# Two-layer decoder trunk (gated linear attention, then sparse attention) on one core: products ahead of the first weights, grouped activation functions, other pacing of the top-k, and embedding blocks and last-head values in other places

## The chip, the cores and the metric

The kernel runs on one core of a Trainium2 chip. The time is the device time of one execution in microseconds (us). Three executions of the kernel before took 2016.35, 2017.49 and 2019.79 us; their median is 2017.49 us.

The engines of the core work side by side, each in the order in which its instructions were issued: PE (TensorE, matrix products), ACT (ScalarE, activation functions and copies), DVE (VectorE, elementwise work), POOL (GpSimd) and SP (SyncE, which here only issues DMAs). They wait for one another through semaphores.

## The reference

Two layers over 1024 tokens of width 1024, in float32. Cut to what matters here:

```python
# layer 0: gated linear attention, 4 heads, chunks of 64 tokens
h = x @ w_in                                   # q, k, v, z, a
g = log_sigmoid(a @ w_a2 + b_a) / 16           # decay per channel
G = cumsum(g, within a chunk)
q_t, k_t = q * dk**-0.5 * exp(G), k * exp(-G)
o = tril(q_t k_t^T) v + q_t S                  # S carried from chunk to chunk
y0 = (rms(o) * gn_g * silu(z)) @ w_out
# layer 1: an indexer scores all keys, 256 of them are kept, 16 heads
score = sum_h relu(qi_h . ki) * wi_h           # causal
idx   = top_k(score, 256)
o     = softmax(q k[idx]^T * scale) v[idx]
y1    = (o * silu(z)) @ w_out
# behind each mixer
x = LayerNorm(alpha * x + y_i)
x = x + (p[i] @ W_ple) * sigmoid(x @ W_gate)
```

## The kernel before

**Numbers.** Nearly every operand of a product is split into a high part (rounded to fp32r) and a low part (the rest), and a product is three matmuls: hi·hi, hi·lo, lo·hi. `split` makes the high part on ACT (L403) and the low one on DVE (L395). The weights are loaded from HBM into "wst" and split into "whi" (ACT, L180) and "wlo" (DVE, L182) by the class `Weights` (`W`), in the order of the list `seq`; `take` hands out the next pair. Weights that are used in both halves of the tokens are split once, ahead, by `split_ahead` (ACT L219, DVE L223, through "pst" and "phi") into HBM, and loaded whole later (`whi<-whs`).

**Stages.** The 1024 tokens are worked in two halves of 512. For layer 0, a half runs through four heads: v, a, z, q and k projections, the decay (`g_phase`), the chunks (`core_steps`), and the output product (`out_phase`), then the normalization and `tail`: transposes of y, the embedding product p W_ple ("ple", 8 blocks of 6 matmuls 128x512), and 8 gate blocks of 24 matmuls. Behind half 0 of layer 0 stand keys, values and the indexer (`small_head`, `index_steps`, `small_kv`). Layer 1 has 17 slots in a half (plan of `slots()`): in slot h the scores S of head h+1 are made, and the values ("o", `pv`) of head h are summed, between projections ("q", "z") and output products ("o" units) that fill PE. The last output units (`last_outs`), the normalization and `tail` end the half.

**What sets the order.** The program is written in the order of the matmuls. `Flow` keeps a clock `now` that counts the columns of the matmuls issued so far at 2.4 GHz. Everything else is put on a heap with a due time (`at`, `after`, `chain`, `spread`) and issued when the clock passes it; `need` runs the heap until something is there. Three pacers run beside it: `W` (a step of the weights every 1.15), `bg` (the top-k and others, a step every `gap`), and `bg3` (`split_ahead`). So the due times fix the order on ACT, DVE and SP, and a wait at run time holds all that stands behind it on its engine.

**The places that the change touches:**
- Start (L1177 on): the first loads and splits of x and of the v weights. `ident` (L356) is the identity that transposes use.
- `g_phase` (L511): on ta [128, 2, 512], per half of the channels Exp (L513), Ln (L514), then a scan; `decays` is another Exp (L539, L541, L542) for the two halves. `z_phase` uses Silu (L602). A change of function set puts an ACT_TABLE_LOAD ahead of the activation.
- `accumulate` (L734) adds an output product into y on DVE (L760, L762) and calls `norm` per token block in its second pass: `stats` (two bn_stats of 512 columns, L803, and bn_aggr, L804), POOL's power for 1/std, and `apply` (L808).
- `load_p` loads the half's p and splits it behind `wait`.
- Index stage: `rl` (L1022, ACT) is the relu of an index product "ix", `sc` (L1016, L1018, DVE) its weighted sum; `zz` (L984) a value evacuation that PE's transposes `U<-ident,zz` wait for; `feed_by` the x splits of half 1.
- Top-k (`topk_steps`): a search by bits, one step every 1.6. A step is a count on DVE (L1040, "tk" or "tkj") or ACT (L1084). At the last bit three score tiles are loaded back (`sc<-sc_s`, L1077) and counted on DVE at 768, 896 and 1024 columns.
- `attend`: `parts` makes ph and PT (the high and low probabilities, L1481 ACT and L1479 DVE), `inverse` and `to_all` bring 1/sum to all partitions by way of HBM (`row`, L1499, and `inv<-row`, L1507), and `pv`, in its last group, multiplies z by inv (L1524), then the values by z (`uf`, L1533), and splits uf into the u of the output product (L403, L395).

Of the kernel before, what the change touches and what calls it, by code (L numbers as in the profile page):

```python
# [23 lines left out]
HT = 512  # L24
NK = 8
# [112 lines left out]
class Weights:  # L138
# [15 lines left out]
    def step(self):  # L154
# [110 lines left out]
def trunk_kernel(ctx, tc, x_tok, x_T, p_T, pos, freq, g_q, g_k, g_v, g_z, g_a, g_a2, g_ba, g_gn, g_o,  # L265
# [28 lines left out]
    def tail_keys(layer):  # L294
        return ([(("p", layer, c), ple_c[layer, c]) for c in range(2)]
                + [(("t", layer, b), gate_c[layer, b]) for b in range(NK)])
# [36 lines left out]
    last_outs = [("o", (6,), 1), ("o", (7,), 0), ("o", (7,), 1)]  # L333

    def unit_keys(u):
        if u[0] == "o":
# [157 lines left out]
    def g_phase(u, A):  # L494
# [16 lines left out]
        def soft(d):  # L511
            def f():
                act.activation(ta[:, d], ta[:, d], AF.Exp, scale=-1.0)  # L513
                act.activation(ta[:, d], ta[:, d], AF.Ln, bias=1.0)  # L514
            return f
# [29 lines left out]
        chain((0, lambda: None), (0.6, soft(0)), (1.1, soft(1)), (0.3, scan(0)), (1.1, scan(1)),  # L545
              (0.8, middle), (1.9, decays))
# [193 lines left out]
    def accumulate(parts, U, y, ch, rs=None, norm=None, ahead=1):  # L740
# [5 lines left out]
        for t, b in order:  # L746
# [16 lines left out]
            if norm is not None:  # L763
                norm(t)
            yield

    def out_phase(u, y, norm=None):
# [4 lines left out]
        for ch in range(2):  # L772
            parts = [W.take(("o", u["h"], ch, 0)), W.take(("o", u["h"], ch, 1))]
            for i, _ in enumerate(accumulate(parts, U, y, ch, u["rs"], norm if ch else None)):
# [14 lines left out]
    def norm_steps(y, np_, eps):  # L789
# [6 lines left out]
        def norm(t):  # L796
# [3 lines left out]

            def stats():
                for c in range(2):
                    dve.bn_stats(st8[:, t, c], y[:, t, c * 512:c * 512 + 512])  # L803
# [944 lines left out]
```

## Time and profile before

| | |
|---|---|
| three runs | 2016.35, 2017.49, 2019.79 us |
| the profiled execution | 2016.59 us, of which the span is 2014.8 us |
| TensorE clock granted, mean | 0.993 |
| share of the span in 40 slices | PE 9 tenths or more in all but two (8) |
| POOL busy | 53.7 us (3%) |
| ACT_TABLE_LOADs | 57 |

A row of the trace's timeline reads: start and duration in us, engine, line, operation, output<-input, shape, how many instructions it holds, and in brackets the idle time that the engine had ahead of it and what ended that wait. The durations of matmuls overlap, so what one costs is the distance between starts. A row of the view by lines has busy us and mean ns behind the bar.

### The profile page before, as it was taken

To read this page: it belongs to the slowest core of one execution; us is meant where nothing else is said; L and a number is where in the kernel's file an instruction comes from. 1 tells how busy PE (TensorE), PEld (TensorE's weight loads), DVE (VectorE), ACT (ScalarE), POOL (GpSimd) and SP (SyncE) were. 2 spreads that over 40 slices of the span, in tenths; PEclk is the share of its full clock that TensorE was granted. 3 is DMA by queue.
4 is the path that set the end of the run, shared out by engine and by line. 5 is a ranking of instruction groups with operands and counts; after the bars stand their busy time and mean duration, and the time that the engine had idled before them with its cause. 6 is when DMAs were issued, how large, how long until landed. Compare 5 with 4: busy or idle time off the path is not lost.

```text
span 2014.8 us, 26716 instructions
## 1 busy us (share of the span) xinstructions
PE 1963.4 (97%) x9016; PEld 1616.3 (80%) x9016; DVE 1487.6 (74%) x3037; ACT 1046.5 (52%) x1943; POOL 53.7 (3%) x111
## 2 busy tenths in 40 slices
PE   8999999999999999999999999999899999999999
PEld 6788788877777888888888887888778888888877
DVE  5667666687677797877867986777796887777863
ACT  5664646445465646464555676766442553434432
POOL 0000000010000000000100000000000000000000
PEclk9999999999999999999999999999999999999999
DMA  4557575657856565657667487877766998888864
GB/s 149 174 162 221 171 218 171 222 174 243 283 180 224 161 225 167 225 162 224 196 218 266 157 311 246 303 265 276 271 211 215 352 333 295 291 300 279 295 249 147
DMA packets 173947, 464.96 MB, mean 231 GB/s; under 512 B 20081, under 2 KB 20849, under 8 KB 167665
## 3 DMA queue, kind: packets, MB, share of 16 engines
q1 hardware_dynamic: 173808, 463.25, 68.4%
q8 instruction: 71, 1.16, 0.2%
q14 instruction: 68, 0.55, 0.1%
HBM read 331.18 MB, written 131.99 MB: 230 GB/s over the span
## 4 chain that ended last, share of the span: by engine, by line
PE 81%; DVE 7%; ACT 5%; DMA 4%; issue 2%; SPq 0%; POOL 0%; POOLq 0%; ACTq 0%; DVEq 0%
PE pb L58 59%; PE o L58 8%; PE U L58 6%; PE S L58 5%; DMA xst<-x2s 1%; DMA wls<-pst 1%; DMA pst<-in_d_o 1%; DVE bn L803 1%; PE oT L62 1%; PE tr L58 1%; DVE wlo L182 1%; DVE sc L1018 1%; ACT whi L180 0%; DMA wst<-in_g_v 0%; DMA wlo<-wls 0%
## 5 line engine op out<-in xcount | busy, mean ns | idle before, releaser
L58 PE MATMUL pb<-x,whi 128*128 128x512 f32 x2272 | 709.9, 394 | 3.3 <-ACT whi L180 2.0
L58 PEld LDWEIGHTS pb<-x,whi 128*128 128x128 f32 x2272 | 417.2, 188 | 84.4 <-ACT whi L180 2.8
L58 PE MATMUL pb<-x,wlo 128*128 128x512 f32 x1136 | 444.2, 391 | 0.4 <-DVE wlo L182 0.4
L58 PE MATMUL pb<-whi,u 128*128 128x512 f32 x1024 | 347.2, 399 | 7.6 <-DVE u L395 4.2
L58 PEld LDWEIGHTS pb<-x,wlo 128*128 128x128 f32 x1136 | 213.8, 188 | 48.1 <-DVE wlo L182 2.3
L58 PEld LDWEIGHTS pb<-whi,u 128*128 128x128 f32 x1024 | 194.8, 190 | 49.9 <-DVE u L395 5.0
L58 PE MATMUL pb<-wlo,u 128*128 128x512 f32 x512 | 202.3, 395 | 0.0
L182 DVE TENSOR_TENSOR wlo<-wst,whi 128x512 fp32r<-128x512 f32 x232 | 154.8, 684 | 56.2 <-ACT whi L180 56.0
L180 ACT ACTIVATE whi<-wst 128x512 fp32r<-128x512 f32 x232 | 136.4, 621 | 47.2 <-DMA wst<-in_g_z 13.7
L219 ACT ACTIVATE phi<-pst 128x512 fp32r<-128x512 f32 x130 | 81.4, 626 | 126.2 <-DMA pst<-in_d_z 40.8
L1435 ACT ACTIVATE sq<-P,mx 128x128 f32<-128x128 f32 (+7 forms) x128 | 99.0, 774 | 83.8 <-DVE mx L1428 56.5
L1481 ACT ACTIVATE ph<-PT 128x512 fp32r<-128x512 f32 (+1 forms) x160 | 93.7, 601 | 65.7 <-PE o L58 50.4
L58 PE MATMUL S<-kT,q 128*128 128x512 f32 (+2 forms) x576 | 121.8, 343 | 0.0
L1479 DVE TENSOR_TENSOR PT<-PT,ph 128x512 fp32r<-128x512 f32 (+1 forms) x160 | 101.5, 648 | 20.6 <-ACT ph L1481 20.6
L58 PEld LDWEIGHTS S<-kT,q 128*128 128x128 f32 x576 | 100.6, 188 | 17.8 <-DVE mx L1428 0.7
L58 PEld LDWEIGHTS pb<-wlo,u 128*128 128x128 f32 x512 | 97.6, 191 | 18.8
L223 DVE TENSOR_TENSOR pst<-pst,phi 128x512 fp32r<-128x512 f32 x130 | 89.1, 685 | 29.8 <-ACT phi L219 29.8
L1084 ACT ACTIVATE tk<-sc,tki 128x768 f16<-128x768 f32 (+2 forms) x90 | 92.9, 1032 | 22.0 <-DVE tki L1093 15.9
L58 PE MATMUL o<-ph,vT 128*128 128x512 f32 (+2 forms) x384 | 102.4, 351 | 0.0
L1441 DVE STREAM_TRANSPOSE sq<-sq 128x128 f32<-128x128 f32 (+7 forms) x128 | 97.6, 768 | 3.1 <-ACT sq L1435 3.0
L58 PE MATMUL pb<-whi,x 128*128 128x512 f32 x256 | 89.1, 407 | 10.0 <-ACT whi L180 6.0
L709 ACT ACTIVATE junk<-o 128x512 bf16<-128x512 f32 x32 | 19.1, 597 | 139.8 <-DVE ot L707 135.3
(311 smaller groups left out, 3383.9 us busy)
## 6 DMA issues: line engine op xcount, KB each, us to landing
whi<-whs SPq DMA_DIRECT2D x130, 512.0 KB
wlo<-wls SPq DMA_DIRECT2D x130, 512.0 KB
sqd<-sq SPq DMA_DIRECT2D x192, 256.0 KB
PT<-sqd SPq DMA_DIRECT2D x48, 1024.0 KB
whs<-phi SPq DMA_DIRECT2D x130, 256.0 KB
wls<-pst SPq DMA_DIRECT2D x130, 256.0 KB
wst<-in_g_v SPq DMA_DIRECT2D x32, 512.0 KB
wst<-in_g_z SPq DMA_DIRECT2D x32, 512.0 KB
```

The source lines that it names most:

```text
L58: self.pe.matmul(out, lhsT, rhs, start=start, stop=stop)
L62: self.pe.transpose(out, in_, ident)
L180: self.nc.scalar.activation(hi[:, c], st[:, c], AF.Copy, scale=1.0 if gain is None else gain)
L182: self.nc.vector.tensor_sub(lo[:, c], st[:, c], hi[:, c].bitcast(F32))
L219: self.nc.scalar.activation(hi, st.bitcast(F32), AF.Copy)
L223: self.nc.vector.tensor_sub(st, st.bitcast(F32), hi.bitcast(F32))
L803: dve.bn_stats(st8[:, t, c], y[:, t, c * 512:c * 512 + 512])
L1084: act.activation(junk()[:, :n], scs[j], AF.Sign, bias=cand[:, j:j + 1].bitcast(F32), accum_out=cnt[:, j:j + 1])
L1435: act.activation(to, rows, AF.Exp, scale=-1.0, bias=mx, accum_out=sm[:, t:t + 1])
L1441: dve.transpose(x, x)
L1479: dve.tensor_sub(lo, lo.bitcast(F32), hi.bitcast(F32))
L1481: chain((0, lambda: act.activation(hi, lo.bitcast(F32), AF.Copy)), (0.8, second))
```

## The change

At the start, 22 products of the identity with itself (128x128, into a PSUM tile that nothing reads) are put ahead of the first weights on PE, and four weight steps stand ahead of the second x split. The rest of the first head is in the same order on PE.

In `g_phase` the two Exp stand together, and so do the two Ln, and later steps are due 1.8 later in all. In its 8 uses 16 of the 57 table loads go: before, ACT has load, Exp, load, Ln twice over, with a weight split (`whi<-wst`) behind each Ln; now it has load, Exp x2, weight split, load, Ln x2, weight split. Rows of ACT further on in head 0, from the last step of the rotary tables (`R`) over the decay block (`mid`, `ta`, `m`) to the next z, before:

```order
L884 ACTIVATE R_100<-R_100 128x1024
L180 ACTIVATE whi<-wst 128x512
L539 ACT_TABLE_LOAD
L539 ACTIVATE mid<-mid 128x8
L541 ACTIVATE ta<-m 128x512
L542 ACTIVATE m<-m 128x512
L541 ACTIVATE ta<-m 128x512
L542 ACTIVATE m<-m 128x512
L180 ACTIVATE whi<-wst 128x512
L602 ACT_TABLE_LOAD
```

and of the changed kernel:

```order
L903 ACTIVATE R_100<-R_100 128x1024
L181 ACTIVATE whi<-wst 128x512 x2
L544 ACT_TABLE_LOAD
L544 ACTIVATE mid<-mid 128x8
L546 ACTIVATE ta<-m 128x512
L547 ACTIVATE m<-m 128x512
L546 ACTIVATE ta<-m 128x512
L547 ACTIVATE m<-m 128x512
L607 ACT_TABLE_LOAD
```

The weight split that stood behind the decay block now stands ahead of it.

In the index stage of half 0 the weights are due 6 later and the x splits of half 1 begin two blocks later and are 1.6 apart instead of 1.2. Rows of ACT there, before:

```order
L954 ACTIVATE u<-zz 64x512 x2
L948 ACTIVATE zz<-pb 128x512
L180 ACTIVATE whi<-wst 128x512 x2
L1022 ACTIVATE rl<-ix 128x384 x3
L954 ACTIVATE u<-zz 64x512 x2
L1022 ACTIVATE rl<-ix 128x384 x2
L970 ACTIVATE zz<-pb 128x512
```

and of the changed kernel:

```order
L973 ACTIVATE u<-zz 64x512 x2
L967 ACTIVATE zz<-pb 128x512
L1041 ACTIVATE rl<-ix 128x384 x3
L973 ACTIVATE u<-zz 64x512 x2
L1041 ACTIVATE rl<-ix 128x384 x2
L181 ACTIVATE whi<-wst 128x512
L989 ACTIVATE zz<-pb 128x512
L1041 ACTIVATE rl<-ix 128x384 x2
```

The two weight splits that stood ahead of the first relu stand behind it.

At the end of a half of layer 1, four things are changed. A new unit ("p",) computes the first two embedding blocks (12 matmuls) between the last output units, with weights split into the two "wst" buffers and p loaded one slot sooner. The product z·inv is made with the last pv group but one. In half 1 the pv of the last head are due 8.6 to 12.8 behind the slot's start. And the unit (7, 0) now has its products ahead (`ahead=3`), so that those of head 14 stand in front of those of head 15. Rows of PE at the end of half 1 (q<- are embedding products, o<- the values, whi,u the output products), before:

```order
L58 MATMUL o<-ph,vT_9801 128x4x64
L58 MATMUL o<-ph,vT_9802 128x4x64
L58 MATMUL o<-PT,vT_9801 128x4x64
L58 MATMUL o<-ph,vT_9801 128x4x64
L58 MATMUL o<-ph,vT_9802 128x4x64
L58 MATMUL o<-PT,vT_9801 128x4x64
L58 MATMUL pb<-whi,u 128x512
L58 MATMUL pb<-wlo,u 128x512
L58 MATMUL pb<-whi,u 128x512 x2
```

and of the changed kernel:

```order
L58 MATMUL o<-ph,vT_9822 128x4x64
L58 MATMUL o<-ph,vT_9823 128x4x64
L58 MATMUL o<-PT,vT_9822 128x4x64
L58 MATMUL o<-ph,vT_9822 128x4x64
L58 MATMUL o<-ph,vT_9823 128x4x64
L58 MATMUL o<-PT,vT_9822 128x4x64
L58 MATMUL pb<-q,wst 128x512 x9
L58 MATMUL pb<-whi,u 128x512
L58 MATMUL pb<-wlo,u 128x512
L58 MATMUL pb<-whi,u 128x512 x2
```

Behind the last values there were output products of head 15; now 9 embedding products and 9 output products of head 14 stand there. In half 0 it is 6 and 9. Rows of DVE at the end of half 0 (tk<-sc counts of the top-k, uf the product of values and z), before:

```order
L1479 TENSOR_TENSOR PT<-PT,ph 128x4x96
L1040 TENSOR_SCALAR tk,tkf<-sc_9808,tki 128x640
L1479 TENSOR_TENSOR PT<-PT,ph 128x2x4x64
L1040 TENSOR_SCALAR tk,tkf<-sc_9809,tki 128x768
L1524 TENSOR_TENSOR z<-z,inv 128x512
L1533 TENSOR_TENSOR uf<-o,z 128x4x4x32
L1040 TENSOR_SCALAR tk,tkf<-sc_9810,tki 128x896
L395 TENSOR_TENSOR q<-xst,q 128x512 x2
L395 TENSOR_TENSOR u<-uf,u 128x512
```

and of the changed kernel:

```order
L1504 TENSOR_TENSOR PT<-PT,ph 128x4x96
L1059 TENSOR_SCALAR tk,tkf<-sc_9830,tki 128x768
L1550 TENSOR_TENSOR z<-z,inv 128x512
L1504 TENSOR_TENSOR PT<-PT,ph 128x2x4x64
L1059 TENSOR_SCALAR tk,tkf<-sc_9831,tki 128x896
L1563 TENSOR_TENSOR uf<-o,z 128x4x4x32
L398 TENSOR_TENSOR u<-uf,u 128x512
L767 TENSOR_TENSOR y<-pb,y 128x512
L806 BN_STATS bn<-y 128x6
```

z·inv stands one group sooner, the splits of p (q<-xst) are gone from there, and the count of 896 columns stands ahead of uf, behind which it stood.

The rest: bn_stats of a block's first 512 columns moves to the first pass of `accumulate` (in all four normalizations); p of layer 0 goes into a buffer of its own and is split 7.0 behind its load; the last head of layer 0 also waits for "late" before its output; the top-k's step is 1.52 at first, then per slot 1.75 (slots 4, 5, 8, 9, 12, 13) or 1.5; behind the last pv of head 15 it pauses for 5; in `tail` the remaining embedding blocks have the transposes of y in pairs behind them. On SP the load of p leaves the last slot, and `sc<-sc_s` of 768 columns stands ahead of `inv<-row`.

The diff, cut:

```diff
-            self.parts[n] = tuple(self.pool.tile([128, 1024], F32R, tag=t, name=t, bufs=4) for t in ("whi", "wlo"))
+            tags = (("wst", 2),) * 2 if self.seq[n][0][:3] == ("p", 1, 0) else (("whi", 4), ("wlo", 4))
+            self.parts[n] = tuple(self.pool.tile([128, 1024], F32R, tag=t, name=t, bufs=b) for t, b in tags)
...
-    last_outs = [("o", (6,), 1), ("o", (7,), 0), ("o", (7,), 1)]
+    last_outs = [("o", (6,), 1), ("p",), ("o", (7,), 0), ("o", (7,), 1)]
...
+        def exps():
+            for d in range(2):
                 act.activation(ta[:, d], ta[:, d], AF.Exp, scale=-1.0)
...
-        chain((0, lambda: None), (0.6, soft(0)), (1.1, soft(1)), (0.3, scan(0)), (1.1, scan(1)),
-              (0.8, middle), (1.9, decays))
+        chain((0, lambda: None), (0.6, exps), (1.2, logs), (2.2, scan(0)), (0.7, scan(1)),
+              (1.0, middle), (1.9, decays))
...
+            dve.bn_stats(st8[:, t, ch], y[:, t, ch * 512:ch * 512 + 512])
+
             def stats():
-                for c in range(2):
-                    dve.bn_stats(st8[:, t, c], y[:, t, c * 512:c * 512 + 512])
                 dve.bn_aggr(mv[:, t], st8[:, t])
...
-            chain((0, stats), (2.0, apply))
+            if ch:
+                chain((0, stats), (1.8, apply))
...
+        turns = iter(range(NK))
+        for b in range(done, 8):
+            if b % 4 == 0 or b == done:
+                parts = first if b < 4 and first else W.take(("p", layer, b // 4))
+            yield from ple_block(parts, b % 4, Pt, ple[b], dve if b >= 4 else act)
+            if b >= 4 + done // 2:
+                for _ in range(2):
+                    xpose(next(turns))
                     yield
+        for k in turns:
+            xpose(k)
+            yield
...
-            W.step()
+            fl.need(lambda: X.t[0] is not None)
+            for _ in range(4):
+                W.step()
             next(feeder)
             feed_by(feeder, 0.0, 0.0)
+            idle = pp.tile([128, 512], F32, tag="o", name="o")
+            for _ in range(22):
+                nc.tensor.matmul(idle[:, 0:128], ident, ident, start=True, stop=True)
...
+        ta = lp.tile([128, 2, HT], F32, tag="e1", name="pt")
+        Pt = load_p(0, half, lambda: t2k("ah", F32R, 4), 7.0, lambda k: ta[:, k])
...
+            W.due = max(W.due, fl.now + 6.0)
...
-                    if i == 8:
-                        feed_by(nxt[2], fl.now + 0.7, 1.2)
+                    if i == 10:
+                        feed_by(nxt[2], fl.now + 0.7, 1.6)
...
-                (ph, pl), *z = get(("parts", h, g), *([("z", h), ("inv", h)] if last else []))
+                (ph, pl), = get(("parts", h, g))
...
+                if g == len(groups) - 2:
+                    z, inv = get(("z", h), ("inv", h))
+                    dve.tensor_mul(z, z, inv)
+                    st["zs", h] = z
                 if last:
-                    dve.tensor_mul(z[0], z[0], z[1])
-                    st["zs", h] = True
+                    z = st["zs", h]
+                    if h == 15:
+                        bg.due = max(bg.due, fl.now + 5.0)
...
-        bg.set(topk_steps([4, 5, 6, 7], scs, l1, tk, tk, on_act=(1, 2, 3)), 1.6)
+        bg.set(topk_steps([4, 5, 6, 7], scs, l1, tk, tk, on_act=(1, 2, 3)), 1.52)
...
+    def ple_unit(st):
+
+        st["pw"] = W.take(("p", 1, 0))
+        st["ple"] = [small_tile("qf") for _ in range(2)]
+        for b in range(2):
+            yield from ple_block(st["pw"], b, Pt, st["ple"][b], act)
+
     def unit(u, norm=None):
         if u[0] == "o":
-            return dsa_out(st, u[1], u[2], y, norm, 3 if u == last_outs[1] else 1)
+            return dsa_out(st, u[1], u[2], y, norm, 3 if u == last_outs[2] else 1)
...
+            bg.gap = 1.75 if h > 3 and h % 4 < 2 else 1.5
...
-                spread(pvs, start + lead + 2.9, dur - lead - 2.4)
+                if h == 15 and half:
+                    spread(pvs, start + 8.6, 4.2)
+                else:
+                    spread(pvs, start + lead + 2.9, dur - lead - 2.4)
...
-            if h == 15:
-                Pt = load_p(1, half, lambda: small_tile("q", F32R, 4), 14.0)
+            if h == 14:
+                Pt = load_p(1, half, lambda: small_tile("q", F32R, 4), dur + 2.5,
+                            lambda k: xp.tile([128, HT], F32, tag="xst", name="xst", bufs=2))
```

More of the change, by code (lines that the diff above doesn't have):

```diff
@@ L294, in tail_keys @@
     def tail_keys(layer):
-        return ([(("p", layer, c), ple_c[layer, c]) for c in range(2)]
+        return ([(("p", layer, c), ple_c[layer, c]) for c in range(layer, 2)]
                 + [(("t", layer, b), gate_c[layer, b]) for b in range(NK)])
@@ L773, in out_phase @@
             parts = [W.take(("o", u["h"], ch, 0)), W.take(("o", u["h"], ch, 1))]
-            for i, _ in enumerate(accumulate(parts, U, y, ch, u["rs"], norm if ch else None)):
+            for i, _ in enumerate(accumulate(parts, U, y, ch, u["rs"], norm)):
                 if ch:
@@ L777, in out_phase, with load_p @@
                 yield
-    def load_p(layer, half, alloc, wait=3.0):
+    def load_p(layer, half, alloc, wait, stage):
         P = []
         for k in range(2):
-            st = xp.tile([128, HT], F32, tag="xst", name="xst", bufs=2)
+            st = stage(k)
             nc.sync.dma_start(st, p_T[layer, k, :, half * HT:half * HT + HT])
@@ L810, in apply, with ple_block, tail @@
                 f_done[t] = True
-            chain((0, stats), (2.0, apply))
+            if ch:
+                chain((0, stats), (1.8, apply))
         return norm, f_done
-    def tail(layer, Pt, y, y_done, final, tp, xps, x_alloc, tmp):
-        ple = [tp.tile([128, 4, HT], F32, tag="z", name="ple", bufs=2) for _ in range(2)]
+    def ple_block(parts, b, Pt, out, engine):
+        hi, lo = parts
+        ps = pbank()
+        n = 0
+        for k in range(2):
+            ph, pl = Pt[k]
+            bs = slice(k * 512 + b * 128, k * 512 + b * 128 + 128)
+            for l, r in ((hi, ph), (hi, pl), (lo, ph)):
+                mm(ps, l[:, bs], r, n == 0, n == 5)
+                n += 1
+            if k == 0:
+                yield
+        if engine is dve:
+            dve.tensor_copy(out, ps)
+        else:
+            act.activation(out, ps, AF.Copy)
+        yield
+    def tail(layer, Pt, y, y_done, final, tp, xps, x_alloc, tmp, ple=(), first=None):
+        ple = list(ple)
+        done = len(ple)
+        for c in range(2):
+            t = tp.tile([128, 4, HT], F32, tag="z", name="ple", bufs=2)
+            ple += [t[:, i] for i in range(4)]
         X1 = [None] * NK
@@ L1237, in trunk_kernel @@
             fl.run(*bulk)
-            if h == GH - 1:
-                Pt = load_p(0, half, lambda: t2k("ah", F32R, 4))
-            else:
-                fl.need(lambda: u.get("late"))
+            fl.need(lambda: u.get("late"))
+        ta = lp.tile([128, 2, HT], F32, tag="e1", name="pt")
+        Pt = load_p(0, half, lambda: t2k("ah", F32R, 4), 7.0, lambda k: ta[:, k])
         norm, y_done = norm_steps(y, lp, EPS / ALPHA ** 2)
@@ L1557, in gate_tiles @@
     def gate_tiles(tp):
[L1558 removed]
+        for tag, bufs in (("z", 3), ("rt", 2)):
             for _ in range(bufs):
@@ L1678, in trunk_kernel @@
         tail_gen = tail(1, Pt, y, y_done, lambda b, t, hs=hs: nc.sync.dma_start(out[b * 128:(b + 1) * 128, hs], t),
-                        tp, spsum, lambda k: (next(gx), next(gx)), tmp1)
+                        tp, spsum, lambda k: (next(gx), next(gx)), tmp1, *first)
         fl.run(tail_gen)
```

47 lines of the change are left out of this document (15 added, 32 removed).

## The prediction

> **What bounds the kernel now.** I read the page's busy times first, then the chain that ended last, and then PE's own timeline for its gaps.
>
> ```profile
> span 2014.8 us, 26716 instructions
> PE 1963.4 (97%) x9016; PEld 1616.3 (80%) x9016; DVE 1487.6 (74%) x3037; ACT 1046.5 (52%) x1943; POOL 53.7 (3%) x111
> PE 81%; DVE 7%; ACT 5%; DMA 4%; issue 2%; SPq 0%; POOL 0%; POOLq 0%; ACTq 0%; DVEq 0%
> ```
>
> PE is busy for 1963.4 of 2014.8 us, so idle time is 51.4 us. The change leaves PE's matmuls as they are (and adds 22 small ones), so all it can win is idle time, plus the slow matmuls that follow it. DVE's 74% is an average: where it is full, PE waits for it, and a gain ahead of such a place is given back there. The start shows how slow:
>
> ```profile
> 5.98 0.79 PE L58 MATMUL pb<-whi,x 128*128 128x512 f32 x1 [5.98 <-ACT whi L180]
> 11.20 1.05 PE L58 MATMUL pb<-whi,x 128*128 128x512 f32 x2
> 12.46 0.39 PE L58 MATMUL pb<-whi,x 128*128 128x512 f32 x1
> 15.45 0.39 PE L58 MATMUL pb<-whi,x 128*128 128x512 f32 x1
> ```
>
> From 11.20 to 12.46 three matmuls take 1.26, 0.42 each; from 12.46 to 15.45 thirteen take 2.99, 0.23 each. So a matmul costs 0.23 with PE warm and 0.42 with PE cold, and a gap of a few us brings the cold spacing back (it is seen again at 561 and 1455 below). Losses are therefore counted as wait plus about 0.2 for each cold matmul behind it. The sum is made against this execution (2016.59 us, span 2014.8); it lies 0.9 under the median of 2017.49.
>
> **Start.** The identity is ready when this ends, at 1.32:
>
> ```profile
> 1.09 0.23 DVE L356 TENSOR_SCALAR ident<-negs 128x128 f32<-128x128 int32 x1 [1.09 <-POOL negs L354]
> 10.73 0.69 DVE L395 TENSOR_TENSOR x<-y,x 128x512 fp32r<-128x512 f32 x1 [0.35 <-ACT x L403]
> ```
>
> No row shows a 128x128 product in full f32; it is taken as one 128x512 fp32r matmul, between 0.23 and 0.42. The 22 then end between 6.4 and 10.6. If PE is warm when the first weights are used, the first 12 matmuls are held by the low part of the fourth x tile (10.73+0.69 = 11.4), and the next 12 follow at 0.23: the pass ends at about 14.4 instead of 15.45, **-1.0**. If it stays cold throughout, the first pass begins at 10.6, has four cold matmuls until 12.46 and 20 warm ones: 17.1, **+1.7**. Range -1.4 to +1.7. [...]
>
> **Table loads.**
>
> ```profile
> L513 ACT ACT_TABLE_LOAD x16 | 20.5, 1283 | 0.3
> 60.01 0.73 PE L58 MATMUL pb<-x,whi 128*128 128x512 f32 x2 [0.86 <-ACT whi L180]
> 59.35 0.61 ACT L180 ACTIVATE whi<-wst 128x512 fp32r<-128x512 f32 x1
> 64.42 0.73 PE L58 MATMUL pb<-x,whi 128*128 128x512 f32 x2 [1.11 <-ACT whi L180]
> ```
>
> Sixteen loads of 1.283 are 20.5 us of ACT, but ACT is busy for 52% only, and PE waits for an ACT held by them just in head 0 of half 0: 0.86 and 1.11. There two loads (2.6 us) go from the queue and the second split leaves its place behind the decays, so both waits should vanish: **-2.0** (0 to -2.6, the loads' own time). In the other heads the loads lie beside PE's products and give nothing.
>
> **Normalization.** Each of four loses four bn_stats from its second pass, 4 x 0.679 = 2.7 us of DVE:
>
> ```profile
> L803 DVE BATCH_NORM_STATS2 bn<-y 128x6 f32<-128x512 f32 x32 | 20.4, 679 | 0.0
> 454.63 0.77 PE L62 MATMUL U<-ident,y 128*128 128x128 f32 x5 [0.87 <-DVE y L808]
> 1472.72 0.81 DVE L808 TENSOR_SCALAR y<-y,mv,rstd 128x1024 f32<-128x1024 f32 x1 [0.44 <-POOL rstd L799]
> 1488.14 0.50 PE L58 MATMUL pb<-gx,whi 128*128 128x512 f32 x1 [0.48 <-DVE gx L395]
> ```
>
> At 454.63 PE waits 0.87 for y; that goes: **-0.9** (0 to -1.5). In layer 1 half 0 y ends at 1473.53 and the x pipeline behind it is late up to 1488.14. y comes 2.7 sooner, but 2.7 us of embedding products (12 x 0.23) leave this place and no longer cover it; the gate blocks, which wait for x tile by tile, gain about **-2.3** (0 to -4). In half 1, where the tail loses almost nothing now, the gate starts sooner relative to x, which ACT supplies: **+0.6** (0 to +2).
>
> **Index stage, half 0 of layer 0.**
>
> ```profile
> 543.66 0.62 PE L58 MATMUL ix<-v,u 128*128 128x384 f32 x2 [2.51 <-ACT rl L1022]
> 542.08 1.15 ACT L180 ACTIVATE whi<-wst 128x512 fp32r<-128x512 f32 x2 [4.27 <-DMA wst<-in_g_v]
> 561.54 0.75 PE L62 MATMUL U<-ident,zz 128*128 128x128 f32 x4 [2.81 <-ACT zz L984]
> 561.95 0.77 PE L58 MATMUL pb<-whi,x 128*128 128x512 f32 x1
> ...
> 565.46 0.63 PE L58 MATMUL pb<-whi,x 128*128 128x512 f32 x2
> 540.00:562.00 22.00, 15.77 (x62) 11.24 (x60) 18.23 (x33) 14.47 (x28) 0.00 (x0) 0.92 0.62 210
> 562.00:570.00 8.00, 8.00 (x30) 6.52 (x29) 7.86 (x16) 5.74 (x12) 0.00 (x0) 0.79 0.68 240
> ```
>
> The relus that PE's next index product needs stand behind two splits that wait 4.27 for a DMA. In the new order they stand ahead. Of 2.51 + 2.81 waited, and 1.7 for eight cold matmuls (from 561.95 to 565.46 they take 3.5 instead of 1.8), 7.0 could go. But the windows (columns: PE, PEld, DVE, ACT, POOL) show DVE busy 18.23 of 22 and then 7.86 of 8: it can be 3.8 us sooner at most unless the later x splits take work out of its way. I take **-3.8** (0 to -7).
>
> **Top-k pace.**
>
> ```profile
> 1229.94 0.50 PE L58 MATMUL o<-PT,vT 128*128 128x512 f32 x1 [2.16 <-DVE PT L1479]
> 1402.09 0.27 PE L62 MATMUL S<-ident,sm 128*4 128x128 f32 x1 [1.73 <-DVE sm L1487]
> ```
>
> Both stalls lie in slots 4 and 12, which now have a step every 1.75 instead of 1.6; 11 of the other slots go to 1.5. With two cold stretches of about 0.5, both gone would be -4.8; new ones elsewhere may cost 3. I take **-2.0** (+3 to -4.8).
>
> **End of half 0, layer 1.**
>
> ```profile
> 1450.56 0.50 PE L58 MATMUL pb<-whi,u 128*128 128x512 f32 x1 [1.98 <-ACT u L403]
> 1455.44 1.22 PE L58 MATMUL pb<-whi,u 128*128 128x512 f32 x2 [4.15 <-DVE u L395]
> 1459.45 0.73 PE L58 MATMUL pb<-whi,u 128*128 128x512 f32 x2
> 1449.15 0.69 DVE L1533 TENSOR_TENSOR uf<-o,z 128x512 f32<-128x512 f32 x1
> 1452.43 1.15 DVE L1040 TENSOR_SCALAR_CACHE_REDUCE tk<-sc,tki 128x896 f16<-128x896 f32 x1 [2.58 <-DMA sc<-sc_s]
> 1454.71 0.68 DVE L395 TENSOR_TENSOR u<-uf,u 128x512 fp32r<-128x512 f32 x1
> 1441.08 0.33 SPq L1507 DMA_DIRECT2D inv<-row  x1
> 1442.88 1.34 SPq L1077 DMA_DIRECT2D sc<-sc_s  x2
> ```
>
> PE waits 1.98 + 4.15, and nine matmuls from 1455.44 to 1459.45 take 4.0 instead of 2.1: 8.1 in all. The low part of u stood behind a count that waited 2.58 for its scores. Now 15 matmuls, 3.4 us, stand between the last values and the first product of head 15, and z·inv is done before. With uf right behind the values (they end near 1448), u's parts are there 2.3 later, under the cover. Against it, the count of 896 is now ahead of uf; its load is issued right behind `inv<-row` (1.4 sooner than the 1442.88 of before) with two weight loads fewer in front. Behind a count that waits stand uf, u's low part and the additions into y, and PE has no more than the 3.4 us before it waits for them. I allow 1.5 for that and for PT's low part behind the counts: **-6.6** (-2 to -8.1).
>
> **End of half 1.**
>
> ```profile
> 1938.02 0.39 PE L58 MATMUL o<-PT,vT 128*128 128x256 f32 x1 [0.62 <-DVE PT L1479]
> 1940.21 0.50 PE L58 MATMUL pb<-whi,u 128*128 128x512 f32 x1 [1.44 <-ACT u L403]
> ```
>
> Here 0.62 + 1.44 and about 1.8 of cold matmuls, 3.9, are covered by 18 matmuls (4.1). The values come 15 matmuls sooner, between output products, and may wait for PT: I allow 1.4, **-2.5** (0 to -3.9).
>
> **What stays, and what costs nothing.**
>
> ```profile
> 639.09 0.49 PE L58 MATMUL tr<-ta,m 128*128 128x128 f32 x2 [3.21 <-DVE m L589]
> ```
>
> It hangs on a DMA of the weights split ahead, whose place in the order is the same: 0 (-4.6 with its cold matmuls if the shift ahead of it takes it away). The rest I cost at nothing. The first embedding weights go into the two "wst" buffers, but in layer 1 the other weights come whole from HBM and need neither these buffers nor a split, so nothing queues behind them. The load of p moves from the last slot to the one before: two DMAs leave SP's queue between `row` and `inv<-row` and stand a slot sooner, where SP is not waited for; if `inv` came late through them there, it would be a wait as in the first rival. The wait for "late" in layer 0 leaves PE's order as it was, and p's own buffer there takes two splits (4 x 0.7 us of ACT and DVE) out of the output product's way, under PE's products.
>
> **Sum:** -1.0 -2.0 -0.9 -2.3 +0.6 -3.8 -2.0 -6.6 -2.5 = -20.5. 2016.59 - 20.5 = 1996.1 for such an execution, 1997.0 beside the median. I forecast **1996.5**.
>
> **Rivals.**
> 1. The count takes uf's place in the wait: if its scores land no sooner than before (1452.43), uf ends at 1454.3 and u's low part at 1455.6, as now, and half 0's end gains 2 instead of 6.6. For it: the row 1452.43. Against: the earlier issue. Time 2001. Chance 0.17.
> 2. DVE gives the gains back: index stage, tail and top-k (3.8 + 2.3 + 2.0) end where they ended because DVE is full there. Time about 2005. Chance 0.15.
> 3. The products at the start are cold to the end (+1.7 instead of -1.0), so that the sum is -17.8: 1999. No row tells whether such products warm PE as the ordinary ones do. Chance 0.1.
> 4. Nothing much: the tight ends wait for other things (PT, `inv`), 2014 to 2019. Chance 0.08.
> 5. Slower: the pace of 1.5 in 11 of 17 slots makes DVE late for PT and sm there. A stall like that at 1229.94 costs 2.16 and some 0.9 of cold matmuls, 3.1; from seven of them on the sum is above zero, and ten give 2027. For it: DVE's 74%, and 1.6 already stalls in two slots. Against: those two hold output products with their own additions, which the other slots lack. Chance 0.05.
>
> The forecast itself has 0.45. The range that leaves out 2 in 10 runs from 1985 (index stage and top-k whole, the stall at 639 gone) to 2009. Measurements of this kernel can tell about 0.2% (4 us) from no change: faster than 2013.5 has 0.87, same 0.08, slower 0.05.
>
> **What would show it.** In the changed profile: no wait for whi near 60 and 64; relu rows ahead of the splits near 540 and no wait of 2.5 there; at the end of half 0 no gap between the embedding products and head 15's, and the count of 896 not waiting for a DMA; fewer cold matmuls there. Wrong it is if new waits for PT or sm stand in the slots of pace 1.5, or if PE is idle for 45 us or more.

## The result, and the profile after

The changed kernel takes 1999.51 us (median of four runs, 1998.01 to 2000.74), the kernel before 2018.64 in the same comparison (2016.35 to 2022.6): ratio 0.9903, 95% interval 0.9884 to 0.9921. The forecast was 1996.5, range 1985 to 2009. The profiled execution took 1998.01, its span is 1996.2 us, 18.6 under the 2014.8 of before; the sum had said 20.5. The page, parts 1 and 4 (the share behind a name in part 4 is its share of the chain):

```profile
span 1996.2 us, 26797 instructions
PE 1961.0 (98%) x9060; PEld 1616.0 (81%) x9060; DVE 1491.3 (75%) x3037; ACT 1022.2 (51%) x1927; POOL 51.4 (3%) x111
...
PE 79%; DVE 8%; ACT 5%; DMA 4%; issue 2%; SPq 1%; POOL 0%; POOLq 0%; ACTq 0%; DVEq 0%
```

PE's idle time is 35 us instead of 51, ACT is busy 24 us less, DVE about as long as before. PE is still the bound. Of the 16 us of idle time, 4.6 are only the products that now fill the wait for the first weights (5.98 us before, 1.38 after). Another part of the gain shows in the trace's record of the granted clock. Behind its first rise it is at half in seven stretches of the kernel before (from 411.8, 544.9, 562.0, 640.5, 1231.0, 1452.9 and 1941.0 us), in which PE is busy for 24.7 us, and in two of the changed kernel (from 405.8 and 545.7), with 6.6. With the prediction's spacings of 0.23 and 0.42, these 18.1 us are worth about 8 (18.1 times 1 - 0.23/0.42; an estimate): nearly half of the gain is cold matmuls.

That the total came out says little about the terms. To read them, the same operation is looked up in both traces, at the borders of the stages: PE's m and oT rows, ACT's first zz of the indexer, DVE's uf of heads 0 and 14. First before, then after, in the order of time:

```profile
42.52 0.73 PE L58 MATMUL pb<-x,whi 128*128 128x512 f32 x2 [0.65 <-DVE m L509]
234.14 0.50 PE L58 MATMUL pb<-whi,x 128*128 128x512 f32 x1 [0.75 <-DVE m L509]
512.72 0.60 ACT L932 ACTIVATE zz<-pb 128x512 f32<-128x512 f32 x1 [1.43 <-PE pb L58]
595.85 0.73 PE L58 MATMUL pb<-x,whi 128*128 128x512 f32 x2 [0.63 <-DVE m L509]
967.98 0.66 PE L62 MATMUL oT<-ident,ot 128*128 128x128 f32 x4 [0.82 <-DVE ot L707]
1166.25 0.69 DVE L1533 TENSOR_TENSOR uf<-o,z 128x512 f32<-128x512 f32 x1 [1.29 <-PE o L58]
1433.63 0.69 DVE L1533 TENSOR_TENSOR uf<-o,z 128x512 f32<-128x512 f32 x1 [0.24 <-PE o L58]
1580.67 0.69 DVE L1533 TENSOR_TENSOR uf<-o,z 128x512 f32<-128x512 f32 x1 [0.86 <-PE o L58]
```

```profile
41.32 0.73 PE L58 MATMUL pb<-x,whi 128*128 128x512 f32 x2 [0.65 <-DVE m L512]
227.20 0.50 PE L58 MATMUL pb<-whi,x 128*128 128x512 f32 x1 [0.75 <-DVE m L512]
506.04 0.60 ACT L951 ACTIVATE zz<-pb 128x512 f32<-128x512 f32 x1
589.44 0.74 PE L58 MATMUL pb<-x,whi 128*128 128x512 f32 x2 [0.65 <-DVE m L512]
958.70 0.66 PE L62 MATMUL oT<-ident,ot 128*128 128x128 f32 x4 [0.82 <-DVE ot L712]
1157.87 0.69 DVE L1563 TENSOR_TENSOR uf<-o,z 128x512 f32<-128x512 f32 x1 [1.50 <-PE o L58]
1420.51 0.69 DVE L1563 TENSOR_TENSOR uf<-o,z 128x512 f32<-128x512 f32 x1 [0.96 <-PE o L58]
1562.54 0.69 DVE L1563 TENSOR_TENSOR uf<-o,z 128x512 f32<-128x512 f32 x1 [0.85 <-PE o L58]
```

The difference of each pair, and of that what the stage added:

| up to | difference | the stage's part | forecast |
|---|---|---|---|
| m of head 0, 42 us (start) | -1.20 | -1.2 | -1.0 |
| m of head 1, 234 us (table loads, decays) | -6.94 | -5.7 | -2.0 |
| first zz, 513 us (normalization of half 0) | -6.68 | +0.3 | -0.9 |
| m of half 1, 596 us (index stage) | -6.41 | +0.3 | -3.8 |
| oT, 968 us (the stall at 639) | -9.28 | -2.9 | 0 |
| uf of head 0, 1166 us (tail of half 1) | -8.38 | +0.9 | 0 |
| uf of head 14, 1434 us (top-k pace) | -13.12 | -4.7 | -2.0 |
| uf of head 0, half 1, 1581 us (end of half 0) | -18.13 | -5.0 | -8.9 |
| the end (end of half 1) | -18.6 | -0.5 | -1.9 |

Only the start came out near its size. The end of half 0 has little over half of its forecast, the other large terms are off by more than a factor of two, up or down, and the misses cancel: that the sum came out is luck.

Each row rests on one trace of each kernel. How far a stage moves on its own shows in the variants below that leave it alone: the start (with its products) ends between 40.5 and 41.9 us; the stretch to the first zz takes 278.2 to 279.8, the index stage (to PE's m) 81.9 to 84.2, the tail of half 1 199.2 to 199.3, the top-k stretch 262.1 to 263.1, the end of half 0 142.0 to 142.4 and that of half 1 94.2 to 94.8. So the two +0.3 are no measured effect.

### The profile page after: what moved, and what is told of

Same layout as the page of the kernel before. It is cut to its first block, busy times and chain, and to the rows that moved or that the text cites. A ratio compares the mean times of both kernels' runs of the same rounds, so it can differ in the third digit from the quotient of the medians.

```text
span 1996.2 us, 26797 instructions
## 1 busy us (share of the span) xinstructions
PE 1961.0 (98%) x9060; PEld 1616.0 (81%) x9060; DVE 1491.3 (75%) x3037; ACT 1022.2 (51%) x1927; POOL 51.4 (3%) x111
## 4 chain that ended last, share of the span: by engine, by line
PE 79%; DVE 8%; ACT 5%; DMA 4%; issue 2%; SPq 1%; POOL 0%; POOLq 0%; ACTq 0%; DVEq 0%
PE pb L58 57%; PE o L58 8%; PE S L58 6%; PE U L58 6%; DVE bn L806 1%; DMA wst<-in_g_z 1%; ACT x L856 1%; DVE wlo L183 1%; DVE y L765 1%; DMA PT<-sqd 1%; PE oT L62 1%; DMA pst<-in_d_o 1%; PE tr L58 1%; DVE y L767 1%; DMA xst<-x2s 1%
## 5 line engine op out<-in xcount | busy, mean ns | idle before, releaser
L58 PEld LDWEIGHTS pb<-x,whi 128*128 128x128 f32 x2272 | 417.0, 188 | 81.9 <-DVE m L512 2.1
L181 ACT ACTIVATE whi<-wst 128x512 fp32r<-128x512 f32 x232 | 136.4, 622 | 41.9 <-DMA wst<-in_g_z 12.5
L1103 ACT ACTIVATE tk<-sc,tki 128x768 f16<-128x768 f32 (+2 forms) x90 | 92.8, 1031 | 22.9 <-DVE tki L1112 19.1
L224 DVE TENSOR_TENSOR pst<-pst,phi 128x512 fp32r<-128x512 f32 x130 | 89.0, 685 | 20.2 <-ACT phi L220 20.0
```

What stands on the lines that cost most here:

```text
L58: self.pe.matmul(out, lhsT, rhs, start=start, stop=stop)
L181: self.nc.scalar.activation(hi[:, c], st[:, c], AF.Copy, scale=1.0 if gain is None else gain)
L224: self.nc.vector.tensor_sub(st, st.bitcast(F32), hi.bitcast(F32))
L1103: act.activation(junk()[:, :n], scs[j], AF.Sign, bias=cand[:, j:j + 1].bitcast(F32), accum_out=cnt[:, j:j + 1])
```

## The experiments

The changed kernel with one part undone or moved; except where rounds are told, each time is that of one profiled execution. A stage is read between the same operations as above.

**1 and 2. Which part of `g_phase` makes the 5.7 us.**

In e1 the chain is that of before, with exp and ln of one direction together in `soft`:

```diff
-        chain((0, lambda: None), (0.6, exps), (1.2, logs), (2.2, scan(0)), (0.7, scan(1)),
-              (1.0, middle), (1.9, decays))
+        chain((0, lambda: None), (0.6, soft(0)), (1.1, soft(1)), (0.3, scan(0)), (1.1, scan(1)),
+              (0.8, middle), (1.9, decays))
```

In e2 the loads are four again, the due times stay:

```diff
-        chain((0, lambda: None), (0.6, exps), (1.2, logs), (2.2, scan(0)), (0.7, scan(1)),
+        chain((0, lambda: None), (0.6, soft(0)), (1.2, soft(1)), (2.2, scan(0)), (0.7, scan(1)),
               (1.0, middle), (1.9, decays))
```

> The changed kernel with g_phase as it was before (four table loads, old due times); all else kept. The changed kernel gains 5.7 us between 40 and 100 us, where the prediction had 2.0. Theory A (the table loads hold the ACT queue: PE's waits for whi, and later DVE's wait for the stored rotary table and PE's waits at 87 and 91): the whole 5.7 comes back, span about 2002, and the waits at 58 to 64, 87 and 91 are there again. Rival (the warm-up products or the weight steps at the start shift this stage): less than half of it comes back.

> The changed kernel with four table loads again (Exp, Ln, Exp, Ln), but with the new due times, so that the weight split stays ahead of the decay block. If the two loads that are gone in this head (2.6 us of ACT) make the gain, 3 to 5.7 us of the 5.7 come back. If the order of the weight split makes it, less than 1.5 comes back.

From m of head 0 to m of head 1 it takes 191.6 us before, 185.9 in the changed kernel, 191.3 in e1 and 188.0 in e2. So with the old chain 5.4 of the 5.7 come back, and so do the waits. With four loads but the new due times 2.1 come back, between what the two theories said: of the 5.4, 2.1 are the loads and 3.3 the order. How the order does it shows in ACT's, DVE's and SP's rows of the kernel before, then in those of the changed kernel and of e2:

```profile
63.75 0.61 ACT L180 ACTIVATE whi<-wst 128x512 fp32r<-128x512 f32 x1
64.40 0.69 DVE L182 TENSOR_TENSOR wlo<-wst,whi 128x512 fp32r<-128x512 f32 x1 [3.71 <-ACT whi L180]
65.01 0.75 DVE L887 TENSOR_SCALAR R<-R,fq 128x1024 f32<-128x1024 f32 x1
65.12 0.33 SPq L199 DMA_DIRECT2D wst<-in_g_k  x1
65.78 0.33 SPq L890 DMA_DIRECT2D rope_s<-R  x1
71.71 0.69 DVE L875 TENSOR_SCALAR R<-R 128x1024 f32<-128x1024 f32 x1 [2.92 <-DMA rope_s<-R]
```

```profile
55.43 1.29 DVE L183 TENSOR_TENSOR wlo<-wst,whi 128x512 fp32r<-128x512 f32 x2 [0.45 <-ACT whi L181]
56.64 0.75 DVE L906 TENSOR_SCALAR R<-R,fq 128x1024 f32<-128x1024 f32 x1
57.42 0.33 SPq L909 DMA_DIRECT2D rope_s<-R  x1
```

```profile
59.66 0.33 SPq L907 DMA_DIRECT2D rope_s<-R  x1
```

The split at 63.75 stands behind the decay block. DVE's low part of the same weights waits 3.71 us for it, and behind that, on DVE, stands the product that finishes a rotary table (65.01 to 65.76). SP stores that table at 65.78, over 8 us later than in the changed kernel, where the low parts wait 0.45. (The load of the next weights, which the split lets go as well, is issued before, at 65.12, and is not what holds the store.) DVE then waits 2.92 us for a store of the tables before it writes on one again, and the m and kh that PE waits for at 87.19 and 90.83 come late. In both kernels with the split ahead of the decays, DVE has no such wait (in e2 PE still waits 0.83 for whi, at 64.53). Theory A was right that the waits come back, but the loads are the smaller part of it in this stage.

Over the whole span e1 loses 7.2 us and e2 6.2. The rest lies mostly in head 0 of half 1, which runs the same code: from m of half 1 to oT it takes 372.1 us before, 372.1 and 373.4 in e1 and e2, and 368.4 to 370.7 in the eleven kernels with two loads. PE's wait for m near 639 is 3.2 before and 3.3 and 3.0 in e1 and e2; in the eleven it is 1.9 at most. So the stall at 639 belongs to the table loads too.

**3. The rotary table for k ahead of half 1's loads** (e3).

`rope_tabs` holds the two loads of `rope_s` that stood in `small_kv`:

```diff
+            tabs2 = rope_tabs(0, alloc)
             nxt = start_half(1)
             next(nxt[2])
```

> The changed kernel with the two loads of the rotary table for k (rope_s, 32 rows) issued ahead of half 1's x and weight loads in the index stage instead of behind them. Theory: the index stage gained nothing because DVE now waits 3.04 for this table (at 542.8) where ACT had waited for the weights; without it PE's wait of 3.62 at 546 goes and the stage ends 3 to 5 us sooner. Rival (DVE is full there anyway, so that the gain is given back by 565): less than 1.5.

The rows of the changed kernel on which it rests:

```profile
534.67 0.54 SPq L982 DMA_DIRECT2D v<-rope_s  x1
542.77 0.68 DVE L923 TENSOR_TENSOR rt<-zz,v 32x512 f32<-32x512 f32 x1 [3.04 <-DMA v<-rope_s]
545.97 1.22 PE L58 MATMUL ix<-v,u 128*128 128x512 f32 x2 [3.62 <-ACT rl L1041]
553.73 0.66 PE L62 MATMUL U<-ident,zz 128*128 128x128 f32 x4 [1.67 <-ACT zz L1003]
```

The span is 1994.6. In e3 DVE doesn't wait for the table and PE's wait of 3.62 is 0.96; from the first zz to DVE's first m the stage takes 80.0 us instead of the 82.6 of the changed kernel. The waits for zz stay (1.94), so that the gain of 2.6 lies between what the two theories said. The eight other variants that leave this stage alone (1, 2 and 4 to 9) take 81.1 to 83.4, and f1 and f2 below, which have the table first, repeat the gain.

**4. The top-k at 1.6 again** (e4).

```diff
-        bg.set(topk_steps([4, 5, 6, 7], scs, l1, tk, tk, on_act=(1, 2, 3)), 1.52)
+        bg.set(topk_steps([4, 5, 6, 7], scs, l1, tk, tk, on_act=(1, 2, 3)), 1.6)
...
-            bg.gap = 1.75 if h > 3 and h % 4 < 2 else 1.5
```

> The changed kernel with the top-k at 1.6 throughout, as before. The changed kernel gains 4.75 us in half 0 of layer 1. If the pace makes it, the waits in slots 4 and 12 (2.2 and 1.7 us) are there again and 3.5 to 5 us come back. If another edit or the shift of the stage makes it, less than 1.5 comes back.

From uf of head 0 to uf of head 14 it takes 268.2 us instead of 262.6: 5.6 come back, of which the end of half 0 gives 0.8 again. The span is 2000.3, and both stalls of before are there:

```profile
1221.32 0.50 PE L58 MATMUL o<-PT,vT 128*128 128x512 f32 x1 [2.14 <-DVE PT L1504]
1394.10 0.27 PE L62 MATMUL S<-ident,sm 128*4 128x128 f32 x1 [2.33 <-DVE sm L1512]
```

**5. bn_stats of both halves in the second pass** (e5).

```diff
-            dve.bn_stats(st8[:, t, ch], y[:, t, ch * 512:ch * 512 + 512])
             def stats():
+                for c in range(2):
+                    dve.bn_stats(st8[:, t, c], y[:, t, c * 512:c * 512 + 512])
```

> The changed kernel with both bn_stats of a block in the second pass again, in all four normalizations. If the 2.7 us of DVE that the change takes from each second pass reach PE, 2 to 3 us come back at the end of half 0 of layer 1 (near 1457), and the waits for y at 444 to 454 and 949 to 960 get longer by 1 us or more. Rival (y is bound by the additions, which follow PE's products one by one): layer 0 loses under 0.5 in each half.

Layer 0 loses 1.2 and 1.3 us in its two halves, and waits for y of 1.49 and 1.33 appear. The first is hardly beyond the spread of its stretch (280.0; 278.2 to 279.8 in others), the second clearly (200.5; 199.2 to 199.3). The end of half 0 of layer 1 loses 0.3, that of half 1 0.2, both within the spread. So it is the other way round than expected: the edit is worth what was forecast in layer 0, and nothing that can be seen in layer 1.

**6. The last head's values in half 1 at their old place** (e7).

```diff
-                if h == 15 and half:
-                    spread(pvs, start + 8.6, 4.2)
-                else:
-                    spread(pvs, start + lead + 2.9, dur - lead - 2.4)
+                spread(pvs, start + lead + 2.9, dur - lead - 2.4)
```

> The changed kernel with the last head's values in half 1 spread as in the other slots. The change gains 0.5 us at the end of half 1 and not the 1.9 forecast. Theory: the waits ahead of head 15's products (about 3.9 with the cold matmuls) do go, and 2.7 us of it is given back because the embedding blocks moved ahead of the last output products are missing in the tail. Then with the old places 9 matmuls fewer stand behind the last values and under 1.5 us come back. Rival (the earlier values do it): 2 to 4 come back.

From uf of head 14 to the end it takes 94.8 us; 94.4 in the changed kernel, 95.0 before. So 0.4 comes back, which is within the spread of this stage (94.2 to 94.8) and under the 1.5 of the theory, though a wait of 1.45 for u is there again:

```profile
1925.75 0.50 PE L58 MATMUL pb<-whi,u 128*128 128x512 f32 x1 [1.45 <-ACT u L406]
```

**7. No products at the start** (e8).

```diff
-            idle = pp.tile([128, 512], F32, tag="o", name="o")
-            for _ in range(22):
-                nc.tensor.matmul(idle[:, 0:128], ident, ident, start=True, stop=True)
```

> The changed kernel without the 22 products at the start. If they make the 1.2 us gained there, PE is cold until the next release of its clock, and 1.0 to 1.5 come back by 40 us. If the other order of the first weight splits makes it, under 0.3.

Neither happened: the stage is 0.5 us *shorter* without them. First the changed kernel, then e8:

```profile
1.38 7.58 PE L1209 MATMUL o<-ident 128*128 128x128 f32 x44 [1.38 <-DVE ident L359]
8.71 0.48 PE L58 MATMUL pb<-whi,x 128*128 128x512 f32 x1
14.26 0.39 PE L58 MATMUL pb<-whi,x 128*128 128x512 f32 x1
```

```profile
5.92 0.79 PE L58 MATMUL pb<-whi,x 128*128 128x512 f32 x1 [5.92 <-ACT whi L181]
7.24 1.05 PE L58 MATMUL pb<-whi,x 128*128 128x512 f32 x2
13.75 0.39 PE L58 MATMUL pb<-whi,x 128*128 128x512 f32 x1
```

The 22 products (44 records) do bring the clock up: it first rises at 6.44 us in the changed kernel, at 10.38 in e8 and at 12.43 before, by the trace's record of the granted clock. But they keep PE until 8.71, while in e8 the weights are used at 5.92, and that gives the gain back. In e8 the third product starts at 7.24; the row of before at the same place:

```profile
8.48 1.22 PE L58 MATMUL pb<-whi,x 128*128 128x512 f32 x2 [0.97 <-DVE x L395]
```

So e8 doesn't wait for the low part of x, which alone makes it 1.24 earlier, and its short products begin at 10.54 instead of 12.46. In the twelve profiled kernels that have the products, the first product with weights starts anywhere between 7.73 and 9.11 and the first pass (24 products) ends between 13.35 and 14.65; e8's 13.75 lies within. One run without the products can't tell whether they gain anything on average; the gain against the 15.45 of before needs no more than the earlier x and the time at which the clock rises. Fewer products, which end when the weights come, were not tried.

**8. No embedding unit** (e9: all eight blocks in the tail; the rest kept).

```diff
-    last_outs = [("o", (6,), 1), ("p",), ("o", (7,), 0), ("o", (7,), 1)]
+    last_outs = [("o", (6,), 1), ("o", (7,), 0), ("o", (7,), 1)]
```

> The changed kernel without the unit of two embedding blocks: all eight blocks in the tail, as before; the rest is kept (z.inv early, products of head 14 ahead, values of the last head in half 1 sooner). Theory: the blocks are needed as cover ahead of head 15's products (6 or 9 matmuls, 1.4 or 2.0 us), but leave the tail uncovered, so that they are worth less than that: half 0 is 0.5 to 2.5 slower, half 1 within 1 us of the changed kernel. Rival (they are the main gain): both halves 2 to 5 us slower.

Both were wrong in the same direction: it is *faster*, 1992.2 of span; 4.0 less than the changed kernel, of which the end of half 0 (uf of head 14 to uf of head 0) has 0.7, 141.4 against 142.0, and the end of half 1 1.5, 92.9 against 94.4; the rest lies in stages that the edit doesn't touch. The rows of the changed kernel's end, then e9's place where the cover is missing:

```profile
1939.62 0.81 DVE L813 TENSOR_SCALAR y<-y,mv,rstd 128x1024 f32<-128x1024 f32 x1 [0.71 <-POOL rstd L804]
1940.86 0.78 ACT L856 ACTIVATE x<-S,lngb 128x512 f32<-128x512 f32 x1 [3.50 <-PE S L62]
1950.20 0.76 ACT L856 ACTIVATE x<-S,lngb 128x512 f32<-128x512 f32 x1
```

```profile
1436.06 0.50 PE L58 MATMUL pb<-whi,u 128*128 128x512 f32 x1 [0.90 <-ACT u L406]
```

Behind the last y stand eight x tiles on ACT, one every 1.33 us (1940.86 to 1950.20 for seven), which the gate's products need. At the end of half 1 the row of the last y starts 37.9 us behind uf of head 14 in the changed kernel and 35.6 in e9; from there to the end it takes 56.6 and 57.3. So the 12 embedding products, 2.7 us, make y 2.3 us later where they stand ahead of it, and the tail only 0.7 us longer where they lie beside ACT's tiles. As cover ahead of head 15 they save a wait of 0.90 in half 0, and in half 1 e9 has no wait there.

**9. z·inv with the last group again** (e6).

```diff
-                if g == len(groups) - 2:
-                    z, inv = get(("z", h), ("inv", h))
-                    dve.tensor_mul(z, z, inv)
-                    st["zs", h] = z
                 if last:
-                    z = st["zs", h]
+                    dve.tensor_mul(z[0], z[0], z[1])
+                    z = st["zs", h] = z[0]
```

> The changed kernel with the product z.inv in the last pv group again. In the changed kernel the low part of head 15's u is there at 1439.4 and the first product that needs it starts near 1439.6, so that 0.7 us more on DVE would show as a wait of 0.5 to 0.7 at the end of half 0. If the covering matmuls leave room, nothing comes back.

Nothing comes back; the end of half 0 is 0.7 us shorter (141.3). In the changed kernel z·inv and the count of 768 stand ahead of PT's last low part on DVE, and PE waits 0.75 for it; in e6 0.15:

```profile
1435.28 1.14 DVE L1059 TENSOR_SCALAR_CACHE_REDUCE tk<-sc,tki 128x896 f16<-128x896 f32 x1
1435.41 0.38 PE L58 MATMUL o<-PT,vT 128*128 128x256 f32 x1 [0.75 <-DVE PT L1504]
```

```profile
1432.47 0.38 PE L58 MATMUL o<-PT,vT 128*128 128x256 f32 x1 [0.15 <-DVE PT L1504]
```

**10. Both gains in one kernel** (f1: e3's and e9's edits, five rounds).

> The changed kernel without the unit of two embedding blocks and with the rotary table for k loaded ahead of half 1's x and weights. If both gains of the single runs stand (2.1 at the index stage, 0.65 and 1.65 at the two ends of layer 1), the time is 3 to 5 us under that of the changed kernel: ratio 0.988 or less. If they were run to run differences, the ratio is the changed kernel's, 0.990.

1992.50 us (four executions, 1991.07 to 1995.47), ratio 0.9881, interval 0.9867 to 0.9896; the 0.988 expected is all but reached. It is the fastest kernel of the study; its interval and the changed kernel's still overlap, so that 3 to 5 us is its likely lead and not a proven one. The index stage takes 79.5, the ends 141.35 and 92.8: the stages repeat what e3 and e9 showed.

**11. The x tiles shared between ACT and DVE** (f2: f1 with this, five rounds).

```diff
-            act.activation(X1[k], ps, AF.Identity, scale=lngb[:, layer, 0, k:k + 1],
-                           bias=lngb[:, layer, 1, k:k + 1])
+            if k % 2:
+                dve.tensor_scalar(X1[k], ps, lngb[:, layer, 0, k:k + 1], lngb[:, layer, 1, k:k + 1],
+                                  op0=OP.mult, op1=OP.add)
+            else:
+                act.activation(X1[k], ps, AF.Identity, scale=lngb[:, layer, 0, k:k + 1],
+                               bias=lngb[:, layer, 1, k:k + 1])
```

> The kernel of the run before (no embedding unit, table first), and in the tails every second tile's scaling behind the transposes moved from ACT to DVE. Theory: the ends are bound by ACT's 1.33 us per x tile behind the last normalized y (eight tiles, 10.6 us), so that sharing it takes up to 2 us from each of the four tails, 2 to 6 in all. Rival (PE's own products bound the tail once x is there): under 1 in all.

1999.70 us, ratio 0.9916 (0.9901 to 0.9930): slower than f1. PE now waits for x from DVE, and for the gate's tiles too:

```profile
450.72 0.66 PE L62 MATMUL U<-ident,y 128*128 128x128 f32 x4 [1.14 <-DVE x L857]
1468.82 0.50 PE L58 MATMUL pb<-gx,whi 128*128 128x512 f32 x1 [1.62 <-DVE gx L398]
```

The end of half 0 of layer 1 is 3.7 us longer than in f1, that of half 1 0.3. In f1 there was little to take. Behind the last values of half 1 PE has no wait left, so its own products bound that end, as the rival said. Behind the last values of half 0 it waits for u (0.89), for y (0.29) and for DVE's gx (0.81, 0.44, 0.24), never for ACT's x.

**12. The index stage's old dues on top of f1** (f3).

```diff
-            W.due = max(W.due, fl.now + 6.0)
...
-                    if i == 10:
-                        feed_by(nxt[2], fl.now + 0.7, 1.6)
+                    if i == 8:
+                        feed_by(nxt[2], fl.now + 0.7, 1.2)
```

> The kernel f1 with the index stage's dues as before (weights not held back by 6, x splits from block 8 and 1.2 apart), table first kept. If the order ACT's relus and weight splits stand in is worth what the prediction said, PE's wait of 2.5 for the relu near 535 is there again and the stage is 2 to 4 us longer than f1's. Rival (the stage is bound by DVE and by the loads of half 1, whatever stands first on ACT): under 1.5.

The stage takes 84.5 us instead of 79.5: 4.9 more, over what was expected.

```profile
539.22 1.01 PE L58 MATMUL ix<-v,u 128*128 128x384 f32 x2 [5.23 <-ACT rl L1045]
```

So the new dues are worth 5 us, as soon as the table is there. 2.2 of them lie above the 82.3 us of the kernel before: in f3 the weights that the old order waits for are issued 26.0 us behind the first zz, before 23.8. Against the kernel before, both edits together are worth 2.8.

## Why the prediction came out, and where its steps failed

- **Table loads** (-2.0 forecast, -5.7 measured, beyond the term's own bound of -2.6). Two steps failed. The prediction took PE's two waits for whi, 0.86 and 1.11, as the whole. It had counted the waits on ACT, not what stands behind the moved split: DVE's low part, the product of the rotary table behind it, its store, and DVE's wait for that store. 2.1 are the loads, 3.3 the order (e1, e2); 0.3 came back in neither. And "In the other heads the loads lie beside PE's products and give nothing" is wrong for head 0 of half 1, as the stall at 639 shows below.
- **Index stage** (-3.8, +0.3). The sentence "In the new order they stand ahead" is right, and the order is worth 5 us with the table there (f3). What failed is that no wait was looked for behind it: the two loads of `rope_s` stand behind half 1's loads on SP, and with the weights' wait gone DVE waits 3.04 for them. With the loads put first the stage is 2.6 to 3.1 shorter (e3, f1). The rest fits the fullness of DVE, the forecast's own bound (3.8): in e3 DVE is busy for 20.2 of the 22 us from 533.7 on.
- **Top-k pace** (-2.0, -4.7). Mechanism right, size at the forecast's own bound of -4.8; e4 shows both stalls and 5.6 us. The feared new stalls were one, of 0.86.
- **End of half 0** (-8.9 with its tail, -5.0). The first rival did not come: the count of 896 has no wait for its scores (row at 1435.28). But the 12 embedding products ahead were taken as cover that costs only "2.7 us ... leave this place", and z·inv as free. Each costs 0.7 net (e9, e6; whether the two add up was not run). And the -2.3 for bn_stats took 2.7 us of DVE to lie on PE's way there, while putting them back costs 0.3 (e5). The last y still comes late: PE waits 1.20 for it.
- **End of half 1** (-1.9, -0.5). The waits of 0.62 and 1.44 went, as said; new ones of 0.48, 0.23 and 0.22 for ph and PT are within the 1.4 that was allowed for them. The 2.7 us of products ahead of y gave most of it back: the forecast had their absence from the tail at 0.6, and e9 is 1.5 shorter without the unit.
- **Normalization in layer 0** (-0.9, +0.3). The edit alone is worth 1.2 in half 0, near the forecast, and 1.3 in half 1, which had none (e5). Something else in the change takes it back: with the edit undone the two stretches are 1.5 and 2.2 us longer than before, of which only the second is clear of the spread. In the changed kernel PE waits 0.72 near 444 for an addition into y, where DVE now also has the splits of p; that p's later split is the cause was not tried.
- **Start** (-1.0, -1.2). The products warm PE (the granted clock first rises at 6.44 us, before at 12.43), as the forecast hoped (its third rival did not come), and the pass ends at 14.26, where its warm case had 14.4. What failed is that this was taken as the gain: e8 has no products, stays cold until 10.38 and is not slower.
- **The stall at 639** (0, -2.9). The prediction said that it hangs on a DMA "whose place in the order is the same". The place is, but not the time. The load of "pst" is issued 37.3 to 37.8 us behind m of half 1 in the three kernels with four table loads (before, e1, e2) and 34.8 to 36.1 behind it in the eleven with two. PE's wait is 3.0 to 3.3 in the three; of the eleven it is gone in four, 0.4 in two and 0.55 to 1.9 in five. So most of the 2.9 is the grouping of the functions. What is left between kernels whose order is the same is the landing: the load was there at most 2.9 us after its issue in the changed kernel (624.70, used at 627.56), in e2 after 4.4. First the changed kernel, then e2:

```profile
624.70 0.33 SPq L211 DMA_DIRECT2D pst<-in_d_o  x1
627.56 0.63 ACT L220 ACTIVATE phi<-pst 128x512 fp32r<-128x512 f32 x1 [2.35 <-DVE tkj L1059]
```

```profile
629.19 0.33 SPq L211 DMA_DIRECT2D pst<-in_d_o  x1
633.63 0.63 ACT L220 ACTIVATE phi<-pst 128x512 fp32r<-128x512 f32 x1 [3.94 <-DMA pst<-in_d_o]
```

What decides the landing stays open.

## What to carry to other kernels

When a wait is taken away or an instruction moved, follow what stands behind it on the other engines, down to the DMAs, and ask which load is the next to be late; here new due times were worth 0 behind a late table, and 2.8 us together with the table loaded first. Code that runs in several places has to be followed in each of them: the table loads cost nothing that shows in heads 1 to 3 (from the last oT row of head 0 to that of head 3 it takes 299.55 us before and 299.57 after in half 0, 296.04 and 296.08 in half 1), and 2 us and more in the first head of either half. Work that is moved forward as cover delays all that is behind it: if the end hangs on a chain of another engine, such work is cheaper inside that chain (here 0.7 us in the tail against 2.3 ahead of y). A sum that comes out right is no evidence for its terms; look at each stage between the same two operations.

## What the runs showed of the hardware that wasn't expected

- Products of the identity in full f32 (128x128) appear as two records each (44 for the 22). In the changed kernel the records follow one another every 0.21 us up to 6.44 and every 0.11 from there on, so that a product takes 0.43 and 0.22, near the 0.42 and 0.23 that the prediction took from products of 128x512; 6.44 is where the record of the granted clock has its first rise. In the twelve kernels that begin alike that rise lies between 4.39 and 7.27, and the 22 products take from 6.61 to 7.98 us, so that the start differs by up to 1.4 us from run to run. The seven stretches at half clock in the kernel before last 3.41 us, or 6.83 in one case. What sets the time of a rise was not shown.
- Loads of the same size at the same place in the program (the "pst" above) were used from 2.8 to 4.9 us after their issue (e9 and e7).
- The loads of ACT's tables show no more than their 1.28 us: in the kernel before the activation behind the load starts 0.01 us after its end in 48 of 57 cases, and in the other nine it waits for PE, DVE or a DMA. Two rows of it:

```profile
44.18 1.28 ACT L513 ACT_TABLE_LOAD   x1
45.48 0.63 ACT L513 ACTIVATE ta<-ta 128x512 f32<-128x512 f32 x1
```
